# Where table building and the scan's low-rank products stand in an encoder trunk's order of work

## Chip, cores and metric

One core of one Trainium2 chip. The metric is the device time of one execution in microseconds; the median of three runs stands for a kernel.

## What is computed

A trunk of one layer over two independent inputs (batch 0 and batch 1, each 1024 positions of 1024 channels), with the same weights. Each input is normed, projected once, and the columns of the projection go to two mixers: a bidirectional RWKV-7 scan with data-dependent decay, and differential attention. Both are joined by an output projection, a residual and a norm; a gated feed-forward part with a short convolution, a residual and a norm follow. Cut to what matters here:

```python
x = layer_norm(x)
proj = x @ w_in                                  # columns: r, k, v, low-rank rows, gate | q, k, v
pa = pa + mu0 * (shift_prev(pa) - pa) + mu1 * (shift_next(pa) - pa)
w_log = -softplus(-(w0 + tanh(wd) @ decay_up)) - 0.5     # low-rank products, one per direction
a = sigmoid(a0 + ad @ iclr_up)
kk = heads(k * k_k); kk = kk * rsqrt(sum(kk * kk, -1) + 1e-12)      # key norms
y = scan(r, decay, k, v, -kk, kk * a) + the same backwards
lam = exp(sum(lp[0] * lp[1])) - exp(sum(lp[2] * lp[3])) + lam_init
attn = softmax(q0 k0 + bias) - lam * softmax(q1 k1 + bias)          # bias by relative position
x = layer_norm(ALPHA * x + concat(scan part, attention part) @ w_out)
x = layer_norm(ALPHA * x + ffn(x))
```

## The kernel before

All large products are split in two parts of the operands (`hi` rounded, `lo` the rest) and run as three matmuls each: lines 264 to 266 where the weights are the stationary side, lines 288 to 290 where the activations are. The weights of one block of 128 columns come by one load of 512 KB on SP's queue (line 235, through the helper `ld` at line 79, so every DMA of SP shows line 79); ScalarE makes `hi` (line 248) and GpSimd `lo` (line 251).

The program is traced stage by stage, and a scheduler sorts it by priority and by a simulated time into one order per engine, which every engine and every DMA queue then follows strictly. The stages of `run` for batch 0:

- `consts` and `norm_in(0)`: constants, the input norm of batch 0, its transposes into `xT`.
- `columns`: small loads of per-channel parameters, turned by three transposes into `cols`; and behind them, in the same function, tables that only later parts read. These are zeros for the part of the scratch `td` that the inversion does not write (lines 195 to 201, one memset and eight stores; read first by the scan's second pass), lambda as a column (`lamn`, lines 203 to 215, one load, five small operations and a product on TensorE; read by attention), and the bias row by distance (`frow`, lines 217 to 226: one load, 31 copies on GpSimd, two stores; read by attention).
- `project(0)`: fourteen blocks of columns. Block 12 first, the low-rank rows: `shifted` (ScalarE line 396, VectorE lines 397 and 399), a tanh, a split, and four stores into the scratch `stk`. Then block 13 and the gate, and then r, k, v for each of four pairs of heads. From the third pair on, the input norm of batch 1 is woven in.
- `project_qk(0)`, `project_v(0)`: the columns of attention.
- `scan(0)`: `pass1`, `pass2` and `attention`. They have a better priority than the projections, so that the projections fill what the scan leaves.

`pass1` first loads the up-matrices of decay and iclr (line 485, behind the last load of the input of batch 0) and casts them on VectorE (lines 487 to 489). For each half it reads the low-rank rows back from `stk` (line 501, four loads). Then come its local stages, one for each pair and half, eight in a batch. Each (`local`) scales and squares k, sums the squares per head on TensorE (line 539, the key norms) and takes ln and exp on ScalarE (lines 540 and 541); for either direction it forms the decay from a low-rank product (line 549, then tanh at 551, plus one at 552, a scan at 557, two exponentials at 560 and 562) and the learning rate from another (line 554, tanh at 555), builds the operands `AB` (lines 575 to 587), and multiplies them per chunk (line 580). The product of line 599 closes a local stage. `invert` and `merge` follow for each group.

PSUM for these products comes from `spsum`, which gives out two tags in turn, two buffers each: the key norms take one tag, the product of line 549 the other, that of line 554 the first again. Nothing but the operands orders line 549: it needs the rows from `stk` and the up-matrices, not k.

The large tiles of the projections have the tag `t` with seven buffers (shifted outputs, norm rows, and the tables above), and the weights have `w` with four and `whi` with two.

Of the kernel before, what the change touches and what calls it, by code (L numbers as in the profile page):

```python
# [42 lines left out]
class Trunk:  # L43
# [90 lines left out]
    def columns(self):  # L134

        nc, cp, I = self.nc, self.cp, self.I
# [55 lines left out]
        self.cb = cols[:, 300:344]  # L192
        self.rk = cols[:, rows["r_k"] : rows["r_k"] + 4]
        self.WC = self.cs.tile([P, NPAIR, 2, NC2, 2], F32, name="WC")
        self.td = [[self.scr(f"td{g}{h}", [P, 2, 2, NC2, C]) for h in range(2)] for g in range(2)]
        zt = self.dt("t", shape=(32, 4 * NC2, 32))
        nc.vector.memset(zt, 0.0)
# [22 lines left out]
        for b, lo, hi in T5_RANGES:  # L220
            m = 1023 - hi
            nc.gpsimd.tensor_copy(out=fr[m // 1024][:, m % 1024 : m % 1024 + hi - lo + 1],
                                  in_=rb[:, b : b + 1].to_broadcast([4, hi - lo + 1]))
# [5 lines left out]
    def weights(self, w, c0, nk, width=P):  # L229
        nc = self.nc  # L230
        out = []
        for k0 in range(0, nk, 8):
            n = min(8, nk - k0)
            st = self.dt("w", shape=(P, 8, P))
            self.ld(out=st[:, 0:n, 0:width],
                    in_=w[k0 * P : (k0 + n) * P, c0 : c0 + width].rearrange("(k p) c -> p k c", p=P))
            hi, lo = self.dt("whi", F32R, shape=(P, 8, P)), self.dt("w", F32R, shape=(P, 8, P))
            self.split(*(a[:, 0:n, 0:width] for a in (st, hi, lo)))
            out.append((k0, n, hi, lo))
        return out  # L240
# [147 lines left out]
    def project(self, b, between=iter(())):  # L388

        nc, I, S = self.nc, self.I, self.st[b]  # L390

        def shifted(m, width=P):
            pp = self.proj(m * P, width)
            o = self.dt("t")
            w = slice(0, width)
            nc.scalar.activation(out=o[w], in_=pp[w], func=AF.Copy, scale=self.c0[w, m : m + 1])
            nc.vector.scalar_tensor_tensor(out=o[w, 1:T], in0=pp[w, 0 : T - 1], scalar=self.mu[0][w, m : m + 1],
                                           in1=o[w, 1:T], op0=ALU.mult, op1=ALU.add)
            nc.vector.scalar_tensor_tensor(out=o[w, 0 : T - 1], in0=pp[w, 1:T], scalar=self.mu[1][w, m : m + 1],  # L399
                                           in1=o[w, 0 : T - 1], op0=ALU.mult, op1=ALU.add)  # L400
            return o


        o = shifted(12)
        nc.scalar.activation(out=o[0:64], in_=o[0:64], func=AF.Tanh)
        lh, ll = self.dt("t", F32R), self.dt("t", F32R)
        self.hilo(o, lh, ll)
        S["stk"] = self.scr(f"stk{b}", [4, 4, 32, T])
        for g in range(4):
            self.ld(out=S["stk"][:, g], in_=(lh, ll)[g % 2])  # L410
        gd = shifted(13, 96)
        nc.scalar.activation(out=gd[0:96], in_=gd[0:96], func=AF.Tanh, scale=0.5)
        nc.vector.tensor_scalar(out=gd[0:96], in0=gd[0:96], scalar1=0.5, scalar2=0.5, op0=ALU.mult, op1=ALU.add)
        gup = self.dt("t", shape=(96, 512))
        self.ld(out=gup, in_=I["g_up"][0])
        for key in "rk":
            S[key] = [self.scr(f"{key}{b}_{p}", [P, T]) for p in range(NPAIR)]
        S["va"] = self.scr(f"va{b}", [NPAIR, P, T])
        S["g"] = [self.scr(f"g{b}_{p}", [P, T]) for p in range(NPAIR)]

        def gate():
            for p in range(NPAIR):
                pp = self.dpsum()
                for j in range(2):
                    sl = slice(512 * j, 512 * j + 512)
                    nc.tensor.matmul(pp[:, sl], gup[:, p * P : (p + 1) * P], gd[0:96, sl], start=True, stop=True)
                o = self.dt("t")
                nc.scalar.copy(out=o, in_=pp)
                self.ld(out=S["g"][p], in_=o)

        S["v"] = [S["va"][p] for p in range(NPAIR)]
        for p in range(NPAIR):
            for key, m0 in (("r", 0), ("k", 4), ("v", 8)):
                o = shifted(m0 + p)
                self.ld(out=S[key][p], in_=o)
                if p >= 2:
                    with self.ahead():
                        next(between, None)
            if p == 0:
                gate()  # L440
# [31 lines left out]
    def pass1(self, b):  # L472
        nc, I, S = self.nc, self.I, self.st[b]
        S["ab"] = [[self.scr(f"ab{b}_{g}_{h}", [NC2, 2, P, 4, P]) for h in range(2)] for g in range(2)]
        S["p2"] = [[self.scr(f"p2{b}_{p}_{hn}", [P, 512]) for hn in range(2)] for p in range(NPAIR)]
        with self.tc.tile_pool(name=f"p1{b}", bufs=1) as pool:
            def tl(tag, bufs=1, dt=F32, shape=(P, 512)):
                return pool.tile(list(shape), dt, name=self.nm(tag), tag=tag, bufs=bufs)

            ups = []  # L480
            for j, (name, d) in enumerate((("decay_up", 0), ("decay_up", 1), ("iclr_up", 0), ("iclr_up", 1))):
                raw, tmp = tl("kk", 2), tl("sg", 2, F32R)
                src = I[name][0, d]
                with self.tc.issue_after(self.first_loads.ins) if b == 0 else nullcontext():
                    self.ld(out=raw, in_=bass.AP(tensor=src.tensor, offset=src.offset, ap=[[0, 4]] + [list(a) for a in src.ap]))
                up = tl(f"up{j}", dt=F32R)
                nc.vector.tensor_copy(out=up[0:64], in_=raw[0:64])
                nc.vector.tensor_copy(out=tmp[64:128], in_=raw[64:128])
                nc.vector.tensor_tensor(out=up[64:128], in0=raw[64:128], in1=tmp[64:128].bitcast(F32), op=ALU.subtract)
                ups.append(up)  # L490
            smask = tl("smask")
            nc.vector.memset(smask, 1.0)
            nc.vector.memset(smask.rearrange("p (c t) -> p c t", t=C)[:, :, 0:1], 0.0)
            merges, ins, stk = [], [], []

            def load(n):
                if n % 2 == 0 and n < 4:
                    stk.clear()
                    for j in range(4):
                        st = tl(f"stk{j}", dt=F32R)  # L500
                        self.ld(out=st, in_=S["stk"][j, :, :, 256 * n : 256 * n + 512].rearrange("g r t -> (g r) t"))
                        stk.append(st)
                if n < 4:
                    ts = slice(512 * (n // 2), 512 * (n // 2) + 512)
                    for i in range(2):
                        x = {}
                        for key in "krvg":
                            x[key] = tl(key, 3 if key in "kr" else 1)
                            self.ld(out=x[key], in_=S[key][2 * (n % 2) + i][:, ts])
                        ins.append(x)  # L510

            def gap():
                if len(merges) > 1:
                    next(merges[0], None)

            load(0)
            for n in range(4):
                hn, pp = n // 2, n % 2
                abd = [self.scr(f"abd{n % 3}{i}", [C, 2, 2, NC2, C]) for i in range(2)]
                for i in range(2):  # L520
                    self.local(b, 2 * pp + i, hn, tl, ups, stk, smask, abd[i], ins.pop(0), gap)
                if n > 1:
                    merges.pop(0)
                if n == 3:
                    list(merges.pop(0))
                load(n + 1)
                merges.append(self.merge(tl, pp, hn, abd, self.invert(pp, hn, tl, abd, n % 3)))
            list(merges[0])

    def local(self, b, p, hn, tl, ups, stk, smask, abd, x, gap):  # L530
        nc, S = self.nc, self.st[b]
        pc = slice(p * P, (p + 1) * P)
        k, r, v, g = (x[key] for key in "krvg")

        kk, sq = tl("kk", 2), tl("L")
        nc.vector.tensor_scalar(out=kk, in0=k, scalar1=self.kkc[:, p : p + 1], scalar2=0.0, op0=ALU.mult, op1=ALU.add)
        nc.scalar.activation(out=sq, in_=kk, func=AF.Square)
        pn = self.spsum()
        nc.tensor.matmul(pn, self.bones, sq, start=True, stop=True)
        nc.scalar.activation(out=sq, in_=pn, func=AF.Ln, bias=self.bcol[:, 0:1])  # L540
        nc.scalar.activation(out=sq, in_=sq, func=AF.Exp, scale=-0.5, bias=self.bcol[:, 1:2])
        nc.vector.tensor_tensor(out=kk, in0=kk, in1=sq, op=ALU.mult)
# [2 lines left out]
        for d in range(2):  # L545
            h = hn if d == 0 else 1 - hn
            rv = (lambda a: a) if d == 0 else (lambda a: a[:, ::-1])
            pz = self.spsum()
            nc.tensor.matmul(pz, ups[d][:, pc], stk[d], start=True, stop=True)
            sg, ta = tl("sg", 2), tl("ta", 2)  # L550
            nc.scalar.activation(out=sg, in_=pz, func=AF.Tanh, scale=0.5, bias=self.w0h[:, 4 * d + p : 4 * d + p + 1])
            nc.vector.tensor_scalar(out=sg, in0=sg, scalar1=1.0, scalar2=0.0, op0=ALU.add, op1=ALU.add)
# [592 lines left out]
    def run(self, x0, x1, y0, y1):  # L1145
        self.st = {}
        with self.tc.tile_pool(name="cs", bufs=1) as self.cs:
# [8 lines left out]
            self.tc.cur_priority += 100000  # L1156
            between = self.norm_in(1, x1)
            self.project(0, between)
            self.project_qk(0, between)
            for g in range(2):  # L1160
                turn = self.turn_in(1, g)
# [45 lines left out]
```

## Time and profile before

| | us |
|---|---|
| median of 3 runs | 3681.4 (3679.78 to 3683.65) |
| the profiled execution | 3670.72 |
| its span, first to last instruction | 3668.6 |
| TensorE busy | 3351.0 |
| VectorE busy | 1989.5 |
| ScalarE busy | 1421.3 |
| GpSimd busy | 1307.4 |

The profile is that of one execution. The page gives the busy time of each engine (PE TensorE, PEld its weight loads, DVE VectorE, ACT ScalarE, POOL GpSimd, SP the queue that issues most DMAs). A table of stretches cuts the span into pieces. A list of waits says which instruction an engine stood still for and what released it. A timeline lists instructions in order of time.

### The profile page before, as it was taken

How to read it: one execution, taken by the hardware profiler on the slowest of the kernel's cores; microseconds unless marked ns; L12 is line 12 of the kernel's file. 1: busy time of each engine (PE TensorE's matmuls, PEld its weight loads, DVE VectorE, ACT ScalarE, POOL GpSimd, SP SyncE). 2: the span in 40 equal slices, each digit the busy share in tenths (PEclk: the TensorE clock that was granted, in tenths of full speed). 3: DMA queues.
4: the chain of work that ended last, by engine and by line, in shares of the span. 5: the costliest groups of instructions: out<-in, count | busy, mean ns of one | idle time of the engine just before them, and what ended most of it. 6: DMA issues, size and time to landing. Idle time of an engine off the chain costs nothing.

```text
span 3668.6 us, 51545 instructions
## 1 busy us (share of the span) xinstructions
PE 3351.0 (91%) x18981; PEld 2748.6 (75%) x18981; DVE 1989.5 (54%) x3654; ACT 1421.3 (39%) x2477; POOL 1307.4 (36%) x1407
## 2 busy tenths in 40 slices
PE   5788878999999997788999999998998899999997
PEld 4566666788878875566788888876876688888876
DVE  6388762335557865878633345448686633333122
ACT  3234332443335543444334343325454333333222
POOL 5265431000232345544221111345452622222464
PEclk9999879889899998898999999999999999999999
DMA  5568774333364656666643333767654322222642
GB/s 161 167 201 233 210 200 106 119 94 96 108 197 145 210 200 179 165 164 158 141 126 107 95 106 103 239 210 224 189 184 147 115 75 69 75 69 76 223 172 87
DMA packets 605391, 545.31 MB, mean 149 GB/s; under 512 B 207388, under 2 KB 480012, under 8 KB 605140
## 3 DMA queue, kind: packets, MB, share of 16 engines
q1 hardware_dynamic: 538580, 508.45, 45.4%
q10 hardware_dynamic: 66560, 33.56, 3.8%
q8 instruction: 152, 2.49, 0.3%
q14 instruction: 99, 0.81, 0.1%
HBM read 361.49 MB, written 180.39 MB: 148 GB/s over the span
## 4 chain that ended last, share of the span: by engine, by line
PE 66%; DVE 13%; DMA 9%; ACT 3%; issue 3%; POOL 3%; SPq 3%; ACTq 0%; POOLq 0%; DVEq 0%
PE d L264 10%; PE d L266 10%; PE d L265 10%; PE d L288 5%; PE d L289 5%; PE d L290 5%; PE s L745 3%; PE s L813 3%; PE s L795 3%; SPq L79 3%; PE s L805 2%; DVE N L621 1%; PE s L926 1%; DVE Ntmp L619 1%; PE s L927 1%
## 5 line engine op out<-in xcount | busy, mean ns | idle before, releaser
L251 POOL TENSOR_TENSOR w<-w,whi 128x256 fp32r<-128x256 f32 (+1 forms) x800 | 758.2, 974 | 1291.6 <-ACT whi L248 1160.3
L264 PE MATMUL d<-xh,whi 128*128 128x512 f32 (+1 forms) x2112 | 857.4, 406 | 14.8 <-DVE t L399 6.3
L266 PE MATMUL d<-xh,w 128*128 128x512 f32 (+1 forms) x2112 | 851.9, 403 | 2.1 <-POOL w L251 2.1
L265 PE MATMUL d<-xl,whi 128*128 128x512 f32 (+1 forms) x2112 | 849.1, 402 | 0.6 <-DVE xl L308 0.6
L248 ACT ACTIVATE whi<-w 128x512 fp32r<-128x512 f32 (+1 forms) x536 | 308.0, 622 | 752.1 <-PE d L290 232.6
L264 PEld LDWEIGHTS d<-xh,whi 128*128 128x128 f32 (+1 forms) x2112 | 407.2, 193 | 106.0 <-issue 7.5
L266 PEld LDWEIGHTS d<-xh,w 128*128 128x128 f32 (+1 forms) x2112 | 407.0, 193 | 94.2 <-issue 3.5
L265 PEld LDWEIGHTS d<-xl,whi 128*128 128x128 f32 (+1 forms) x2112 | 407.2, 193 | 91.5 <-issue 2.2
L1078 DVE SCALAR_TENSOR_TENSOR t<-d,cols,t 128x1023 f32<-128x1023 f32 x88 | 112.7, 1281 | 405.9 <-ACT t L1077 405.8
L288 PE MATMUL d<-whi,xh 128*128 128x512 f32 x640 | 259.3, 414 | 36.0 <-DVE t L1058 20.7
L289 PE MATMUL d<-w,xh 128*128 128x512 f32 x640 | 261.4, 408 | 2.1 <-POOL w L251 2.1
L290 PE MATMUL d<-whi,xl 128*128 128x512 f32 x608 | 247.0, 406 | 0.0
L1058 DVE SCALAR_TENSOR_TENSOR t<-t,d 128x512 f32<-128x512 f32 x112 | 72.5, 677 | 242.4 <-PE d L290 239.2
L935 ACT ACTIVATE e<-e,ms 128x1024 f32<-128x1024 f32 x128 | 147.0, 1148 | 138.1 <-DVE ms L933 134.4
L288 PEld LDWEIGHTS d<-whi,xh 128*128 128x128 f32 x640 | 124.3, 195 | 71.9 <-issue 12.5
L942 POOL TENSOR_SCALAR e<-e,ms 128x512 f32<-128x512 f32 x128 | 89.0, 708 | 250.0 <-DVE ms L940 108.7
L749 DVE TENSOR_TENSOR G<-s,ms 64x256 f32<-64x256 f32 x128 | 53.7, 420 | 190.8 <-PE s L745 190.1
L289 PEld LDWEIGHTS d<-w,xh 128*128 128x128 f32 x640 | 124.3, 194 | 32.4 <-POOL w L251 5.4
L813 PEld LDWEIGHTS s<-X,Q 128*128 128x128 f32 x1024 | 134.0, 199 | 10.0 <-DVE X L808 1.8
L290 PEld LDWEIGHTS d<-whi,xl 128*128 128x128 f32 x608 | 118.0, 194 | 28.1 <-issue 1.0
L745 PE MATMUL s<-G,BK 64*128 64x128 f32 x1024 | 138.2, 298 | 0.5 <-ACT Q L759 0.3
L813 PE MATMUL s<-X,Q 128*128 128x64 f32 x1024 | 137.1, 280 | 0.3 <-DVE X L808 0.3
(230 smaller groups left out, 6181.6 us busy)
## 6 DMA issues: line engine op xcount, KB each, us to landing
w<-in_ffn_up SPq DMA_DIRECT2D x88, 512.0 KB
w<-in_ffn_down SPq DMA_DIRECT2D x88, 512.0 KB
h<-t SPq DMA_DIRECT2D x66, 512.0 KB
ab<-AB ACTq DMA_DIRECT2D x64, 512.0 KB
w<-in_w_in SPq DMA_DIRECT2D x58, 512.0 KB
G<-ab SPq DMA_DIRECT2D x128, 128.0 KB
BK<-ab SPq DMA_DIRECT2D x64, 256.0 KB
w<-in_w_out SPq DMA_DIRECT2D x32, 512.0 KB
```

What stands on the lines that cost most here:

```text
L248: nc.scalar.activation(out=hi[:, s], in_=w[:, s], func=AF.Copy)
L251: nc.gpsimd.tensor_tensor(out=lo[:, s], in0=w[:, s], in1=hi[:, s].bitcast(F32), op=ALU.subtract)
L264: nc.tensor.matmul(o, wh, rh, start=first, stop=False)
L265: nc.tensor.matmul(o, wh, rl, start=False, stop=False)
L266: nc.tensor.matmul(o, wl, rh, start=False, stop=last)
L288: nc.tensor.matmul(out[i], lh, wh, start=k == ks[0], stop=False)
L289: nc.tensor.matmul(out[i], lh, wl, start=False, stop=False)
L290: nc.tensor.matmul(out[i], ll, wh, start=False, stop=k == ks[-1])
L745: nc.tensor.matmul(pp[i][:, u * P : (u + 1) * P], BK[st, u], G[i][st, u], start=True, stop=True)
L813: last = nc.tensor.matmul(pv[g][:, i, u], ops[g][3][i][:, u], x[:, s, 1, u], start=False, stop=True, skip_group_check=True)
L935: nc.scalar.activation(out=e_, in_=e_, func=AF.Exp, bias=ms[:, 2 + c : 3 + c], accum_out=ms[:, 4 + c : 5 + c])
L1078: nc.vector.scalar_tensor_tensor(out=o[:, 1:T], in0=pp[:, 0 : T - 1], scalar=self.cw[0][:, m : m + 1], in1=o[:, 1:T], op0=ALU.mult, op1=AL ...
```

## The change

Three edits. The tables behind `columns` become a function of their own, `tables`, which `run` calls behind `project(0)`, with the priority of the projections. In `project`, the last load of weights for the first pair's blocks (that of its v block) is kept as `S["ahead"]`, and the loads of the low-rank rows in `pass1` are queued behind it on SP. In `local`, the product of line 549 is queued on TensorE behind the key norms of its stage. `issue_after(ins)` orders what its block traces on the engine of `ins` behind `ins` in the queue of that engine; it adds no wait. No instruction is added or taken away.

```diff
@@ columns
         self.WC = self.cs.tile([P, NPAIR, 2, NC2, 2], F32, name="WC")
+
+    def tables(self):
+
+        nc, cp, I = self.nc, self.cp, self.I
         self.td = [[self.scr(f"td{g}{h}", [P, 2, 2, NC2, C]) for h in range(2)] for g in range(2)]
@@ weights
-            self.ld(out=st[:, 0:n, 0:width],
+            self.loaded = self.ld(out=st[:, 0:n, 0:width],
                     in_=w[k0 * P : (k0 + n) * P, c0 : c0 + width].rearrange("(k p) c -> p k c", p=P))
@@ project
                 o = shifted(m0 + p)
+                if p == 0:
+                    S["ahead"] = self.loaded.ins
                 self.ld(out=S[key][p], in_=o)
@@ pass1, load
-                        self.ld(out=st, in_=S["stk"][j, :, :, 256 * n : 256 * n + 512].rearrange("g r t -> (g r) t"))
+                        with self.tc.issue_after(S["ahead"]):
+                            self.ld(out=st, in_=S["stk"][j, :, :, 256 * n : 256 * n + 512].rearrange("g r t -> (g r) t"))
@@ local
-        nc.tensor.matmul(pn, self.bones, sq, start=True, stop=True)
+        norms = nc.tensor.matmul(pn, self.bones, sq, start=True, stop=True)
@@ local
-            nc.tensor.matmul(pz, ups[d][:, pc], stk[d], start=True, stop=True)
+            with self.tc.issue_after(norms.ins):
+                nc.tensor.matmul(pz, ups[d][:, pc], stk[d], start=True, stop=True)
@@ run
             self.project(0, between)
+            self.tables()
             self.project_qk(0, between)
```

## Rows read from the trace of the kernel before

**Rows 1.** The page's busy line of TensorE: busy us, share, instructions; then the others.

```profile
PE 3351.0 (91%) x18981; PEld 2748.6 (75%) x18981; DVE 1989.5 (54%) x3654; ACT 1421.3 (39%) x2477; POOL 1307.4 (36%) x1407
```

**Rows 2.** Stretches: from:to, us, busy us of each engine, clock, DMA share, GB/s.

```profile
52.00:64.00 12.00, 12.00 (x61) 9.29 (x60) 4.79 (x15) 2.26 (x5) 0.14 (x1) 1.00 0.72 138
64.00:75.00 11.00, 4.11 (x19) 2.68 (x17) 5.46 (x10) 2.35 (x4) 4.12 (x18) 0.91 0.14 45
75.00:90.00 15.00, 12.93 (x42) 9.64 (x42) 6.02 (x5) 5.32 (x6) 9.09 (x23) 0.72 0.33 97
90.00:107.00 17.00, 0.00 (x0) 0.00 (x0) 0.00 (x0) 0.00 (x0) 0.00 (x0) 0.60 0.43 150
...
95.00:103.00 8.00, 0.00 (x0) 0.00 (x0) 0.00 (x0) 0.00 (x0) 0.00 (x0) 0.50 0.25 100
...
107.00:133.00 26.00, 25.85 (x105) 20.98 (x106) 6.05 (x6) 5.79 (x9) 5.67 (x8) 0.93 0.36 118
...
250.00:300.00 50.00, 42.62 (x216) 33.69 (x215) 49.51 (x74) 18.67 (x26) 28.89 (x28) 0.86 0.74 215
300.00:350.00 50.00, 36.73 (x220) 28.28 (x219) 34.83 (x54) 18.60 (x26) 28.04 (x28) 0.89 0.84 235
```

**Rows 3.** Waits of TensorE, 60 to 115 us: us in total, times, longest.

```profile
PE s L549 <- DMA stk<-stk: 17.2, 1, 17.2
PE d L264 <- DVE t L399: 6.3, 1, 6.3
PE d L266 <- POOL w L251: 1.7, 1, 1.7
```

**Rows 4.** Timeline of SP's queue: start, us of issuing, what is moved, how many.

```profile
53.25 7.95 SPq L79 DMA_DIRECT2D td<-t  x8
...
61.79 1.19 SPq L79 DMA_DIRECT2D kk<-in_iclr_up  x2
...
74.91 0.25 SPq L79 DMA_DIRECT2D frow<-t  x1
75.25 0.41 SPq L79 DMA_DIRECT2D w<-in_w_in  x1
77.45 7.28 SPq L79 DMA_DIRECT2D stk<-t  x4
...
91.16 0.42 SPq L79 DMA_DIRECT2D w<-in_w_in  x1
103.74 1.77 SPq L79 DMA_DIRECT2D stk<-stk  x4
```

**Rows 5.** Timelines of ScalarE, VectorE and GpSimd, 64 to 80 us.

```profile
65.88 1.09 ACT L396 ACTIVATE t<-d,c 128x1024 f32<-128x1024 f32 x1
...
71.27 1.29 DVE L489 TENSOR_TENSOR up<-kk,sg 64x512 fp32r<-64x512 f32 x2
72.59 1.28 DVE L397 SCALAR_TENSOR_TENSOR t<-d,cols,t 128x1023 f32<-128x1023 f32 x1
...
70.88 6.65 POOL L222 COPY t<-t 4x1 f32<-4x1 f32 x31 [18.74 <-DMA t<-in_rel_bias]
```

**Rows 6.** The longest wait of ScalarE, 80 to 115 us.

```profile
ACT sg L551 <- PE s L549: 22.8, 1, 22.8
```

**Rows 7.** Timeline of the first two local stages: decay, next early product, next norms.

```profile
141.18 0.70 ACT L551 ACTIVATE sg<-s,halfc 128x512 f32<-128x512 f32 x1
...
143.90 0.41 DVE L552 TENSOR_SCALAR sg<-sg 128x512 f32<-128x512 f32 x1
...
159.62 0.79 PE L549 MATMUL s<-stk,up 128*128 128x512 f32 x1
...
187.87 1.02 PE L539 MATMUL s<-L,bones 128*128 128x512 f32 x2
188.33 0.80 PE L554 MATMUL s<-stk,up 128*128 128x512 f32 x1
```

**Rows 8.** A wait of TensorE from 1380 to 1860 us, first pass of batch 1.

```profile
PE s L549 <- ACT L L540: 5.9, 1, 5.9
```

## The prediction

> **What bounds the kernel now.** I read the page's busy line first: TensorE is busy for 91% of the span [rows 1], and the work that it does hardly changes here, so the question is where it stands idle. A table of stretches then shows that the first 107 us are the worst part: from 64 to 75 us TensorE works 4.11 of 11 us, from 75 to 90 it works at a mean clock of 0.72, and from 90 to 107 no engine does anything at all [rows 2]. A stretch in which all five engines are empty is time that can be taken out whole, since nothing else fills it. The list of waits says for what TensorE stood still there: 17.2 us before the first low-rank product of the scan (line 549), for the load of its operand; 6.3 us before the third projection, for VectorE's shift (line 399); 1.7 us for GpSimd's split of the weights [rows 3]. The order on SP's queue explains the operand: the low-rank rows are stored from 77.45 us, and the load that reads them back leaves at 103.74, when the store has landed [rows 4]. Line 549 stood ahead of the k projection in TensorE's order, so that a projection whose weights had been fetched from 75.25 us on waited for a product that nobody needed yet. ScalarE, whose queue is in order too, stood 22.8 us behind that product with the split of the next weights behind it [rows 6].
>
> **Part 1: the tables leave the head.** Eight stores of zeros (7.95 us of SP), the load and arithmetic of lambda, the load of the bias table, 31 small GpSimd copies (6.65 us) and two stores of the bias row go from before the first projection to behind its last column block. What goes with them:
> - The two iclr_up loads issue at 61.79 us, right behind the eight stores that begin at 53.25 [rows 4]. VectorE's casts of them end with line 489 at 71.27 + 1.29 us, and only then comes the shift of the first projection, line 397 at 72.59, whose input ScalarE had finished at 65.88 + 1.09 = 66.97 [rows 5]. With the loads some 8 us earlier the casts are done by about 65 and the shift begins at 66.97: 72.59 - 66.97 = 5.6 us, inside the 6.3 us for which TensorE waited. I take **5.6**. Of that wait 0.7 us stays: the shift is then itself what comes last.
> - GpSimd is at the 31 copies from 70.88 to 77.5 us [rows 5] while the split that the third projection needs stands behind them: **1.7 us** [rows 3].
>
> **Part 2: the first low-rank product goes behind the key norms.** Line 549 is now queued behind line 539, which needs k from the projection that it used to hold up. So it can't stand ahead of that projection any more, and its operand is there before it is asked for: **17.2 us** [rows 3]. The whole of it counts, since no engine worked meanwhile [rows 2].
>
> **The clock.** Behind both idle stretches TensorE ran below full speed: 15 us at 0.72 and 26 us at 0.93, after 0.60 in the empty stretch [rows 2]; 0.72 lies between its two levels, 1.2 and 2.4 GHz. If all of that were won back it would be 15 x 0.28 + 26 x 0.07 = 6 us; if a new gap of 2 us keeps the lower level for a time, nothing. I take **3**, the middle.
>
> Sum of the gains: 5.6 + 1.7 + 17.2 + 3 = **27.5 us**.
>
> **What it costs.**
> - **The tables at their new place.** I take it that tiles of one tag are handed out in the order of the program, and so expect them behind the outputs of the last v block, at about 290 us in the old times. The stretch is full: VectorE 49.51 of 50 us before 300, the DMA engines 0.84 from 300 to 350, and TensorE idle 13.3 us of those 50 already [rows 2]. All twelve DMAs stand in SP's queue between weight loads, the stores of the bias row wait for GpSimd's copies, and what is queued behind them on SP waits along: weights, and so TensorE. The lower bound is 0, as the scan does not need the tables before its second pass and a gain is excluded (the stretch loses no work); the upper is both rows one after the other, 7.95 + 6.65 = 14.6 us [rows 4, 5]. I take **5**, nearer to the lower, as TensorE can run one projection ahead there and much of what it waits for is VectorE.
> - **The products behind the norms.** There are 16 local stages (two batches, four steps, two pairs). Until now line 549 ran ahead: at 159.62 us, with its norms at 187.87 [rows 7], so its decay (lines 551 and 552) was done long before it was wanted. Now the product (0.79), ScalarE's line 551 (0.70) and VectorE's line 552 (0.41) lie behind the norms [rows 7], beside the two activations of the norms. Upper bound: 16 x 1.90 = 30 us. Lower bound: -5.9 us, since the early products also made TensorE wait, 5.9 us in the second batch [rows 8]. I take **2**: the decay has until the key is normed, and dense products fill TensorE meanwhile.
> - **Loads behind the weights of the v block.** These stood in that order anyway: the load of v's weights at 91.16, that of the low-rank rows at 103.74 [rows 4]. So the new order on SP only keeps what is there. But the store takes 103.74 - 77.45 = 26.3 us, and with the shift it starts at about 71.8 and lands at 98. By then r is done (69.7 + 12) and k too, at about 93. If v's weights are issued behind the store and wait for it, TensorE stands up to 5 us; if ahead, nothing. I take **2.5**, the middle.
>
> One rule on that store: by the Trainium skill, DMA: Bandwidth & Descriptors, section "Why a DMA increments its semaphore by 16 and not by 1", a copy runs on the largest number of engines up to 16 that divides the slowest dimension of both sides, which is 4 for this store. The row from 95 to 103 us, with nothing else in flight, agrees: a share of 0.25 and 100 GB/s [rows 2]. By the rule the landing stays at 98 and so does the 2.5; were it free to spread, 2 MB at the 235 GB/s of rows 2 would land near 81, and the sum would be 2.5 better.
>
> A rule that speaks against the change: the same page, section "Specifications", asks for at least 512 bytes in a piece, and the zeros are stored in pieces of 128. The rows agree so far: a share of 0.72 for 138 GB/s while they run, 0.84 for 235 later [rows 2]. By it the stores take 0.72 x 12 = 8.6 us of all engines wherever they stand, and the 16% that are free from 300 to 350 are 8 us: estimated so, the price of the new place would be 8.6 and not 5.
>
> **The sum.** 27.5 - 5 - 2 - 2.5 = **18 us**. The profiled execution took 3670.7 us (its span 3668.6 and 2.1 around it), so 3652.7; the median of the runs is 10.7 above that execution, and the same 18 us from 3681.4 give **3663.4**. What the measurement can tell from no change is about 0.2%, 7.4 us.
>
> **The rivals.**
> - **The tables stall the later stretch as they did the head.** For: it is fuller than the head was, and a store that waits for GpSimd holds SP again. Against: the weights are fetched ahead. At 14.6 us and with the clock term gone: 27.5 - 3 - 14.6 - 4.5 = 5.4, **3676**, within 0.2%.
> - **The scan becomes the bound: slower.** Each local stage is a chain over TensorE, ScalarE and VectorE, and VectorE is full from 250 to 300 us [rows 2]. If the 1.90 us of line 549 and its decay come on top of each chain and TensorE waits for it, 30 us go: 27.5 - 5 - 30 - 2.5 = -10, **3691**. It decides from 20 / 16 = 1.25 us per stage on. Against it: TensorE has other work in most of these stages.
> - **It doesn't do what it says.** Only line 549 is tied to the norms; line 554 reads the same kind of operand and isn't. If it is put ahead of the k projection instead, the 17.2 us and 2 of the clock stay: **3682**. Against it: in the trace it runs right behind the norms, at 188.33 after 187.87 [rows 7], and it shares their PSUM tag.
> - **All costs at their lower ends:** 27.5 + 5.9 = 33, **3648**.
>
> **How the numbers follow.** The forecast (3663; its own range 3652 to 3673, the middles of clock, tables, products and loads off by up to 3, 5, 5 and 2.5 us but not all one way) has 0.50, the lower ends 0.10, the later stall 0.17, the scan as bound 0.13, no effect on the wait 0.10. From 3644 to 3688 lie all but the slower case and a few per cent below. Faster: 0.50 + 0.10 + a quarter of the stall = 0.64. Same: the rest of the stall and most of the fourth, 0.21. Slower: 0.15.
>
> **What would show it.** The wait of line 549 for its load gone, and no stretch up to 110 us with all engines empty; the shift of line 397 at about 67 us; the first norms (134 us before) at 105 to 110. Wrong would be: another product waiting for the same load, a gap of over 10 us behind the stores of zeros near 270 us, or TensorE idle longer in either first pass of the scan.

## The result and the profile after

The forecast was 3663.0 us, range 3644 to 3688. The change is slower, and outside that range:

| | before | after |
|---|---|---|
| median, us | 3681.25 (3679.78 to 3683.65, 4 runs) | 3730.99 (3727.94 to 3733.29, 4 runs) |
| ratio | 1 | 1.0134 (95%: 1.0116 to 1.0152) |
| profiled execution: span, mean granted clock | 3668.6, 0.943 | 3726.2, 0.931 |

Lines of after are 4 higher than those of before from about line 195 on, and 7 or 8 higher in and behind `local`: L546 are the key norms (before: 539), L557 the low-rank product that the change ties to them (549), L562 the other one (554), L588 the chunk products (580), L655 the inversion's (647), L217 lambda's product (213), L268 to L270 the dense products of the projections (264 to 266). Each run below has line numbers of its own again.

TensorE's stretches after, to be read against [rows 2]; columns are from:to, us, busy us (instructions), granted clock, DMA share, GB/s:

```profile
52.00:64.00 12.00, 5.28 (x22) 0.86 0.27 93
64.00:75.00 11.00, 11.00 (x42) 0.84 0.05 13
75.00:90.00 15.00, 12.77 (x50) 0.89 0.36 102
90.00:107.00 17.00, 17.00 (x76) 1.00 0.24 99
107.00:133.00 26.00, 14.26 (x34) 0.66 0.56 182
133.00:250.00 117.00, 117.00 (x498) 0.99 0.56 173
250.00:300.00 50.00, 42.67 (x228) 0.93 0.73 219
600.00:700.00 100.00, 55.29 (x632) 0.53 0.46 96
```

and two stretches of before that are not among its rows above:

```profile
133.00:250.00 117.00, 104.38 (x531) 0.99 0.67 203
600.00:700.00 100.00, 87.72 (x541) 0.80 0.42 123
```

The empty stretch from 90 to 107 us is gone, as forecast. Instead TensorE waits before 64 us and from 107 to 133; it is busy without a break from 133 to 250, where before it had gaps; and from 600 to 700 it stands idle for 44.7 us, where before it was 12.3, with the clock near the lower of its two levels (1.2 of 2.4 GHz).

What it did in the full stretch says where the loss begins. TensorE's timeline after, from the first key norms on (start, us, instruction, count, idle time before it and what ended it; `issue` where the profile names no releaser):

```profile
120.79 3.75 PE L430 MATMUL d<-t,t 96*128 96x512 f32 x4 [8.31 <-issue]
127.54 2.08 PE L546 MATMUL s<-L,bones 128*128 128x512 f32 x2 [3.00 <-ACT L L544]
128.63 1.42 PE L562 MATMUL s<-stk,up 128*128 128x512 f32 x1
130.48 3.78 PE L430 MATMUL d<-t,t 96*128 96x512 f32 x4 [0.44 <-ACT t L432]
133.28 1.42 PE L557 MATMUL s<-stk,up 128*128 128x512 f32 x1
...
249.25 0.38 PE L217 MATMUL s<-t,bcol 1*128 1x1 f32 x2
249.55 0.50 PE L557 MATMUL s<-stk,up 128*128 128x512 f32 x1
...
259.84 1.15 PE L588 MATMUL s<-AB 64*64 64x64 f32 x32
```

The first norms run at 127.54, 6.6 us ahead of before (134.1), and line 557 follows for one direction at 133.28. For the other direction the same product runs only at **249.55**, right behind lambda's product at 249.25. The first chunk products come at 259.84, where before they came at 147.72: the scan starts 112 us late. From 138.2 us to lambda's product TensorE does only projections. In SP's queue the load of lambda's parameters stands at 238.50 us, behind the input of batch 1: its tile has the tag `t`, and the program asks for it behind those of the projection.

The waits of TensorE from 0 to 700 us (us in total, times, longest), first the largest of after, then its like in before:

```profile
PE s L655 <- DMA M<-t1d: 45.7, 5, 12.9
```

```profile
PE s L647 <- DMA M<-t1d: 14.1, 2, 12.1
```

At the end of the first pass TensorE waits 45.7 us for the inversion's data, with nothing else to do: the projections that fill those gaps in before have already run, and the next ones aren't let go yet. A helper, `paced`, orders the projections of batch 1 behind marks in the scan of batch 0, so that they run at most a set amount of work ahead of it (50 us). From 133 us to the first norms of batch 1 (1421.5 us before, 1456.7 after) TensorE is idle for 125.1 us before and 159.5 after, which is where most of the loss lies:

```profile
133.00:1421.50 1288.50, 1163.45 (x7207) 0.91 0.57 166
```

```profile
133.00:1456.70 1323.70, 1164.25 (x7185) 0.89 0.56 161
```

### The profile page after: what moved, and what is told of

It reads as the page before. It is cut to its first block, busy times and chain, and to the rows that moved or that the text cites. A ratio compares the mean times of both kernels' runs of the same rounds, so it can differ in the third digit from the quotient of the medians.

```text
span 3726.2 us, 51564 instructions
## 1 busy us (share of the span) xinstructions
PE 3368.0 (90%) x18981; PEld 2767.3 (74%) x18981; DVE 1988.6 (53%) x3654; ACT 1419.2 (38%) x2475; POOL 1308.6 (35%) x1407
## 5 line engine op out<-in xcount | busy, mean ns | idle before, releaser
L268 PE MATMUL d<-xh,whi 128*128 128x512 f32 (+1 forms) x2112 | 856.1, 406 | 9.8 <-ACT whi L252 5.0
L270 PE MATMUL d<-xh,w 128*128 128x512 f32 (+1 forms) x2112 | 842.5, 399 | 0.4 <-POOL w L255 0.4
L268 PEld LDWEIGHTS d<-xh,whi 128*128 128x128 f32 (+1 forms) x2112 | 404.4, 192 | 102.2 <-ACT whi L252 7.9
L270 PEld LDWEIGHTS d<-xh,w 128*128 128x128 f32 (+1 forms) x2112 | 403.6, 191 | 93.4 <-issue 2.4
L943 ACT ACTIVATE e<-e,ms 128x1024 f32<-128x1024 f32 x128 | 147.0, 1149 | 138.4 <-DVE ms L941 119.4
L950 POOL TENSOR_SCALAR e<-e,ms 128x512 f32<-128x512 f32 x128 | 89.3, 711 | 219.2 <-DVE ms L948 124.6
L753 PE MATMUL s<-G,BK 64*128 64x128 f32 x1024 | 146.0, 305 | 10.9 <-DMA v<-va 10.7
L293 PEld LDWEIGHTS d<-w,xh 128*128 128x128 f32 x640 | 124.6, 195 | 31.6 <-POOL w L255 4.0
L753 PEld LDWEIGHTS s<-G,BK 64*128 64x128 f32 x1024 | 121.3, 204 | 31.5 <-issue 22.3
```

The source lines that it names most:

```text
L268: nc.tensor.matmul(o, wh, rh, start=first, stop=False)
L270: nc.tensor.matmul(o, wl, rh, start=False, stop=last)
L293: nc.tensor.matmul(out[i], lh, wl, start=False, stop=False)
L753: nc.tensor.matmul(pp[i][:, u * P : (u + 1) * P], BK[st, u], G[i][st, u], start=True, stop=True)
L943: nc.scalar.activation(out=e_, in_=e_, func=AF.Exp, bias=ms[:, 2 + c : 3 + c], accum_out=ms[:, 4 + c : 5 + c])
```

## Experiments

Each ratio is to before's runs on the same chip, with its 95% interval. "Products behind the norms" is the third edit of the change (lines 549 and 539), "loads behind weights" the second.

**1. Lambda alone moved.** The kernel before with only lambda's lines (203 to 215) traced behind `project(0)`; zeros and bias row stay at the head, and no ordering is added.

> The kernel before, with nothing changed but the place of lambda: its load, its arithmetic and its product go behind the first projection; the zeros, the bias row and both orderings stay as before. Theory A (the product's PSUM tile stands ahead of the scan's tiles of the same tag, so the low-rank product of the first local stage waits for lambda, whose tiles come behind the projection's): the product of lambda and behind it the first low-rank product of direction 0 run at about 250 us, the first chunk products at about 260 instead of 148, and the time is 3725 to 3740, all of the loss of the change. Theory B (the zeros and the bias row stall the stretch where they land, or the orderings lengthen the local stages): 3675 to 3685, as before.

3722.0 us, ratio 1.0102 (1.0077 to 1.0126). Just under the 3725 to 3740 expected. Its TensorE timeline shows the same pair, lambda's product (L227) and the scan's low-rank product (L552):

```profile
247.43 0.38 PE L227 MATMUL s<-t,bcol 1*128 1x1 f32 x2
247.73 0.50 PE L552 MATMUL s<-stk,up 128*128 128x512 f32 x1
```

Moving a load, five small operations and one product (0.38 us, two instructions) is enough for about 39 of the 50 us.

**2. Everything but lambda.** The changed kernel with lambda's lines left in `columns`.

> The changed kernel with lambda left where it was, ahead of the first projection: zeros and bias row move, both orderings stay. Theory A: the loss goes away and what was forecast for the head comes: first norms at 105 to 115 us, no wait for the low-rank rows, 3650 to 3675. Theory B: the loss stays, 3715 to 3735, as zeros, bias row and orderings are all still there.

3687.0 us, 1.0012 (0.9992 to 1.0033): the loss is gone, but what was forecast for the head does not come, so the 3650 to 3675 expected are missed.

**3. Lambda moved, its product in another PSUM tag.** The changed kernel with

```diff
-        pl = self.spsum()
+        self.side = not self.side
+        pl = self.dpsum()
```

so that only the tile's tag differs: `d`, that of the projections. The first of the two lines keeps the turn of the scan's two tags as it was.

> The changed kernel with one thing other: lambda's product writes a PSUM tile of the projections' tag instead of one of the scan's; all tables stay moved. Theory A: the same as with lambda left at its place, 3650 to 3675, since the tag alone was the matter. If it is not the tag but the late arithmetic of lambda: 3725 to 3740.

3680.8 us, 0.9989 (0.9970 to 1.0008): the same miss of 3650 to 3675, and the loss gone again. Lambda's product now runs at 307.9 us, later than ever, and the scan doesn't care (L547 norms, L558 the tied product, now for both directions at once):

```profile
126.19 2.07 PE L547 MATMUL s<-L,bones 128*128 128x512 f32 x2 [2.82 <-ACT L L545]
127.27 1.42 PE L558 MATMUL s<-stk,up 128*128 128x512 f32 x1
128.49 0.63 PE L563 MATMUL s<-stk,up 128*128 128x512 f32 x1
129.13 3.78 PE L431 MATMUL d<-t,t 96*128 96x512 f32 x4
131.92 1.42 PE L558 MATMUL s<-stk,up 128*128 128x512 f32 x1
```

Runs 1 to 3 settle the loss. Tiles of a PSUM tag are handed out in the order in which the program asks for them. Lambda's product asks before the scan, so the scan's first product of that tag can't have a tile until lambda's has had one. The tag has two buffers, one for each of the two products, and line 557 ran right behind lambda's product without waiting for its result to be read: it was held by the order of handing out, not by a lack of room. That the product of the other direction, of the other tag, ran at 133.28 fits.

**4. The tables moved, no ordering.** The changed kernel without its second and third edit.

> The tables moved as in the change, without its two orderings: the low-rank loads aren't held behind weight loads and the products aren't held behind the norms. Theory (lambda's product takes a PSUM tile of the scan's two tags and holds the scan's first direction-0 product behind it): the loss stays whole, 3720 to 3740 us, that product at about 249 us instead of 147.7, and 600 to 700 us as empty for TensorE as in the changed kernel (about 45 us idle). Rival (the loss needs an ordering too, since a product held behind the norms can't run early): 3680 to 3695.

3707.9 us, 1.0082 (1.0054 to 1.0109): about half of the loss stays (26 of 50 us), below the 3720 to 3740 expected, with TensorE busy 56.75 us of the 100 from 600 to 700. The loss does not need the orderings, but they make it some 24 us larger here.

**5. The changed kernel with projections further ahead.**

```diff
-FREE = (50.0, 1e9)
+FREE = (110.0, 1e9)
```

> The changed kernel with the second batch's projections allowed to run 110 us of work ahead of the first batch's scan instead of 50, lambda's product where the change puts it. Theory (the late scan costs what TensorE then lacks in work: the projections are tied to the scan's progress and are not let go while it catches up): TensorE idle from 600 to 700 us about 20 to 35 us instead of 45, and 3700 to 3720. Rival (the loss is the scan's own length from its first product to its end, whatever runs beside it): 3725 to 3740 with the stretch as empty as before.

3701.4 us, 1.0054 (1.0028 to 1.0081). The stretch that was empty is full again:

```profile
600.00:700.00 100.00, 94.47 (x802) 0.91 0.54 131
```

From 133 us to batch 1's first norms TensorE is idle for 135.0 us, against 159.5 in the changed kernel:

```profile
133.00:1428.40 1295.40, 1160.36 (x7171) 0.91 0.56 163
```

So 112 us of late start cost 50 us at the end largely because TensorE ran short of other work while the scan caught up; about 30 of them come back with more work let go. The kernel before was not run with the same 110 us, so how much of the 30 it would win there too is not shown.

**6. Only the two orderings.** The kernel before with the second and third edit.

> The kernel before with the two orderings alone; all tables stay at the head. By the terms of the prediction: the 17.2 us wait goes and about 2 us of the clock come back, less 2 for the later decay and 2.5 for the loads, 3660 to 3672. By theory B (the orderings lengthen each of 16 local stages by up to 1.9 us): 3685 to 3712.

3683.7 us, 1.0001 (0.9984 to 1.0018). Neither range expected (3660 to 3672, 3685 to 3712) has it. The wait of 17.2 us is gone and the first norms come at 125.7 instead of 134.1, with nothing of it at the end. Runs 2, 3 and 6 have this in common, and it opened the second question: where does the gain of the head go?

**7 and 8. The product behind the norms in the first local stage alone**, in the kernels of runs 6 and 2:

```diff
-            with self.tc.issue_after(norms.ins):
+            with self.tc.issue_after(norms.ins) if b == 0 and p == 0 and hn == 0 else nullcontext():
```

> The kernel before with the two orderings, that of the product behind the norms for the first local stage alone (batch 0, first pair, first step); the tables at the head as before. In the run with the ordering in every stage the first norms came 8 us earlier and the second batch's norms 15 us earlier, and the end was not earlier. Theory (the ordering in the later stages gives the head's gain back, in the second batch's first pass and at its attention): 3664 to 3674, with attention of the second batch starting 10 us or more ahead of before. Rival (the gain is lost around the start of the second batch's attention however the stages are ordered): 3680 to 3686.

> The changed kernel with lambda left where it was and the ordering of the products behind the norms for the first local stage alone. Theory (later stages' ordering gives the gain back): the first norms at 120 us as with all stages ordered, second batch's norms some 20 us ahead of before, and 3656 to 3670. Rival (gain lost at the second batch's attention anyway): 3680 to 3688.

3673.9 us, 0.9984 (0.9966 to 1.0001), and 3671.7 us, 0.9977 (0.9958 to 0.9996). Both move the expected way; the first lies at the upper end of its range, the second just above, and only the second interval excludes 1. Batch 1's attention does not start 10 us earlier in run 7, as expected, but at 2480.7 us (before: 2477.4). TensorE's idle time tells how large the head's gain is: up to 133 us it is 54.9 us in before, 47.0 in run 7, 48.8 in run 6 and 46.8 in run 2. That is 6 to 8 us, beside a clock of 0.92 instead of 0.90. In run 7 the medians differ by 8 us too.

**9 and 10. Weights, then k too, ahead of the low-rank loads.** Run 8 with those loads also behind the weights of the next pair's r; then also behind the store of k.

> The one before, with the low-rank loads held behind the weight load of the next pair's r too, so that those weights are not queued behind them on SP. If the 9 us that TensorE waited from 104 to 114 us come from weights queued behind low-rank loads that wait for their store: the first norms at 110 to 114 us and 5 to 9 us less than the run before at all later marks, 3648 to 3664. If they come from ScalarE's and VectorE's order (a split ahead of k's shift): norms at 118 to 121 and the same time as the run before within 3 us.

> As the run before it (lambda where it was, products behind the norms in the first local stage alone, low-rank loads behind the next pair's weights) and the low-rank loads also behind the store of k, so that k too is not queued behind loads that wait for the long store. Theory (whatever stands behind the four low-rank loads on SP waits until the store lands at about 99 us; it was the weights, then the key): the first norms at 109 to 113 us instead of 118 to 120, the first product some 2 us behind, and the end 3655 to 3668. Rival (the key's way to the norms is set by ScalarE's and VectorE's order): norms at 116 to 120 and no less time than 3664 to 3672.

3666.9 us, 0.9973 (0.9955 to 0.9991), and 3668.9 us, 0.9971 (0.9950 to 0.9992): the same as run 8 within the intervals, and run 9 above the 3648 to 3664 expected. The traces show a wait that moves along a queue. SP's queue in run 2, where the low-rank loads come first (start, us of issuing):

```profile
73.23 7.55 SPq L79 DMA_DIRECT2D stk<-t  x4
...
99.31 1.77 SPq L79 DMA_DIRECT2D stk<-stk  x4
101.13 0.43 SPq L79 DMA_DIRECT2D w<-in_w_in  x1
```

and what waited there, on ScalarE:

```profile
ACT whi L252 <- DMA w<-in_w_in: 25.6, 2, 24.3
```

The weights for the next block sit behind loads that wait for the long store, ScalarE's split of them sits ahead of k's shift, and TensorE idles 9.25 us before 113.57. In run 9 the weights go first and TensorE idles 2.1 us there, but 8.5 us before the norms (2.9 in run 2), since VectorE now waits for k, whose load is the one behind:

```profile
DVE kk L543 <- DMA k<-k: 10.4, 1, 10.4
```

In run 10 k is ahead as well; its wait is still 8.1 us, and the norms come at 116.0 (run 8: 120.0, run 9: 118.0). The expectations of 110 to 114 (run 9) and 109 to 113 (run 10) were not met. What won 18 us against before at the first norms is worth 5.8 at the first product of the second pass's chain (line 795 in before; 636.2 against 642.0). TensorE's longest waits from 250 to 600 us (the chunk products, for their operands `AB`), before and run 10, show where the rest went:

```profile
PE s L580 <- DVE AB L576: 26.6, 8, 6.1
```

```profile
PE s L590 <- DVE AB L586: 44.3, 9, 7.6
```

TensorE arrives earlier and waits 17.7 us longer for VectorE's operands; over the whole stretch it is busy for 11.2 us less (277.82 against 289.01).

**11 and 12. The orderings in one batch only**: run 6 with the products behind the norms for batch 0 alone (`if b == 0`; the loads stay behind the weights in both batches), and with both orderings for batch 1 alone.

> The kernel before with the two orderings, the products behind the norms in the first batch only. Theory (the cost of the ordering falls in the second batch's first pass, where TensorE waits for VectorE's decay): from the first batch's attention to the second's 1425 to 1436 us as before, and 3664 to 3676 in all. Rival (the cost is in both batches): 3676 to 3684.

> The kernel before with both orderings in the second batch only, so the head is that of before. Theory: from the first batch's attention to the second's 1440 to 1450 us instead of 1427.6, TensorE idle some 15 us longer between 1390 and 1700, and 3690 to 3700 in all. Rival (the ordering costs nothing there, the head's gain is lost by other means): 3679 to 3686.

3653.9 us, **0.9919** (0.9902 to 0.9937), and 3692.8 us, 1.0025 (1.0009 to 1.0041). The ordering costs in batch 1, 8 to 9 us in run 12, as the theory had it. But batch 0 alone gains 31 us, far more than the 6 to 18 expected. TensorE's order in run 11 is that of run 6, instruction by instruction, up to the first local stage of batch 1: the ordering in batch 1 is all that was taken away, and the two medians differ by 30 us (the two profiled executions by 18). TensorE from 1400 to 1700 us, in before, run 6 and run 11:

```profile
1400.00:1700.00 300.00, 237.71 (x1495) 0.85 0.63 165
1400.00:1700.00 300.00, 223.85 (x1450) 0.84 0.60 156
1400.00:1700.00 300.00, 228.02 (x1433) 0.82 0.63 162
```

and its longest wait there, that of the chunk products for their operands `AB`, in run 6 and in run 11:

```profile
PE s L584 <- DVE AB L580: 45.7, 10, 13.3
```

```profile
PE s L584 <- DVE AB L580: 25.3, 8, 5.9
```

With the ordering, TensorE waits 20 us longer for the operands that come out of the decay: the low-rank product that used to run ahead of the norms now lies behind them, and the decay with it. But other waits make up for most of that, as TensorE is busy for only 4.2 us more in run 11. Stretches cut at the same products, and not at the same times, show where the two part. First batch 1's first pass (first norms to the first product of the second pass), then its attention (first to last product of lines 926 and 927 in before), in before, run 6, run 11 and run 12:

```profile
1421.50:1872.10 450.60, 386.49 (x2790) 0.89 0.60 153
1406.20:1862.40 456.20, 381.16 (x2775) 0.88 0.58 149
1416.30:1862.20 445.90, 373.82 (x2710) 0.87 0.60 150
1431.20:1880.00 448.80, 377.24 (x2771) 0.89 0.61 151
```

```profile
2477.40:2812.00 334.60, 313.74 (x1555) 0.97 0.60 193
2475.50:2816.40 340.90, 319.34 (x1592) 0.97 0.61 192
2450.50:2802.20 351.70, 342.53 (x1725) 0.98 0.64 202
2496.70:2835.40 338.70, 319.57 (x1592) 0.96 0.62 193
```

In the first pass TensorE is idle for 64.1 us in before, 75.0 in run 6, 72.1 in run 11 and 71.6 in run 12. So the ordering in batch 1 is paid there: 7.5 us more in run 12 than before, about what it measured. That pass also takes back what run 6 had won in the head. Run 11 does not get it back there (72.1). Its gain lies in the attention, 9.2 us idle against 21.6 in run 6 and 20.9 in before: more dense products (lines 288 to 290) were left to fill that stretch, 842 against 744 in run 6 and 696 in before. Why the scheduler leaves more of them there is not shown.

**13 to 15. The change without its fault, batch 0 alone.** Run 2, run 3 and run 10 with the products behind the norms in batch 0 only.

> The changed kernel with lambda left where it was and the ordering behind the norms in the first batch alone. With that ordering in both batches it measured 1.0012 of before. Theory (the ordering in the second batch gives the gain back, 9 to 31 us): 3650 to 3668. Rival (the ordering in the second batch matters only with the tables at the head, by the order that the planner then finds): 3676 to 3690, as with both batches.

> The changed kernel with lambda's product in the projections' PSUM tiles and the ordering behind the norms in the first batch alone. With both batches it measured 0.9989 of before. Theory: 3650 to 3668. Rival: 3674 to 3686, as with both batches.

> As the first of these, with the low-rank loads behind the next weights and k's store, which made the first norms come at 116.0 us instead of 120.0. If time won in the first stage reaches the end: 2 to 4 us less than the first of these. If the scan's later stages are held by other work and TensorE just waits for VectorE there (44.3 us instead of 26.6 between 250 and 600 in the run with the first stage alone ordered): the same within 4 us.

3672.2 us, 0.9997 (0.9977 to 1.0017); 3652.5 us, **0.9943** (0.9920 to 0.9965); 3678.0 us, 1.0002 (0.9986 to 1.0018). Run 14 met its expectation, 13 and 15 did not. Leaving the ordering out of batch 1 moved all three pairs the same way (runs 6 to 11: 1.0001 to 0.9919; 3 to 14: 0.9989 to 0.9943; 2 to 13: 1.0012 to 0.9997, which the intervals don't separate), but by 5 to 30 us. Run 15, whose first norms are the earliest of all (115.2), is no faster than run 13 (119.4) and clearly slower than run 11 (126.3). All four kernels with the products ordered in every stage of batch 0 alone (runs 11, 13, 14, 15) have the full attention of run 11: 8 to 10 us idle, against 19 to 24 in the others apart from run 5 (15.5). Run 15 loses it again before: from 133 us to batch 1's first norms TensorE is idle for 139.7 us, against 124.6 in run 11. So a few us won in the first stage are easily outweighed by how the scheduler sorts the later stages. Between runs 11 and 13 the traces show only 3 us of idle time up to the end of that attention, while the medians differ by 18 us: this stays open. Runs 11 and 14 beat both kernels.

## Why the prediction was wrong

**The step that failed** is the cost of the tables at their new place (5 us, bounds 0 and 14.6). It named the rule that did the damage, tiles of one tag are handed out in the order of the program, and applied it to the tag `t` alone. The moved function also asks for a PSUM tile, of the tags that the scan's products use; both lines are in the kernel (212 and 548). Following "the scan does not need the tables before its second pass" was right for the data and wrong for the buffer. By the same, what is said ahead of the prediction, that nothing but its operands orders line 549, does not hold: its PSUM tile orders it too. None of the rivals had it: the bound of 14.6 for this step stands against 45 to 53 us measured (1.0134 against 1.0012 and 0.9989 in runs 2 and 3). Without this fault the forecast would have missed too: those two runs are no faster than before, so the 18 us did not come.

**The head's gains** were 27.5 us in the sum; TensorE's idle time up to 133 us fell from 54.9 to 49.6. By term:
- *The shift, 5.6 us.* The shift was to begin at 66.97 us and begins at 74.95. The iclr loads were indeed earlier (54.71 us), but VectorE's casts moved with them, and two of them, waiting for their load, now stand ahead of the split of batch 0's input that TensorE's first projection needs. VectorE after, and TensorE behind it:

```profile
60.41 0.42 DVE L493 CAST up<-kk 64x512 fp32r<-64x512 f32 x1 [5.87 <-DMA kk<-in_iclr_up]
60.84 0.42 DVE L494 CAST sg<-kk 64x512 fp32r<-64x512 f32 x1
61.30 0.69 DVE L312 TENSOR_TENSOR xl<-s,xh 128x512 fp32r<-128x512 f32 x1
```

```profile
62.05 0.80 PE L269 MATMUL d<-xl,whi 128*128 128x512 f32 x1 [5.00 <-DVE xl L312]
```

  The forecast asked when the casts would be done, not what is queued behind them while they wait. In run 2 short operations of lambda sit there instead, the split runs at 56.93 and the shift begins at 68.35.
- *The copies, 1.7 us.* Right: no wait for GpSimd's split is left there.
- *The wait of line 549, 17.2 us.* It is gone, as are the 22.8 us of ScalarE behind it [rows 6]; instead ScalarE stands 23.4 us for weights. About half of it came back as the gap before the gate's products (8.31 us after, 9.25 in run 2). This is the term "loads behind the weights of the v block", 2.5 us: it looked at v's weights, and the ones that waited were those behind the low-rank loads on SP. The long store itself was as forecast, 26.1 us from issue to the loads behind it (80.18 to 106.25 after, 73.23 to 99.31 in run 2) against 26.3 before [rows 4]. By the Trainium skill, DMA: Bandwidth & Descriptors, section "Why a DMA increments its semaphore by 16 and not by 1", a copy runs on the largest number of engines up to 16 that divides the slowest dimension of both sides, 4 for this store; the unchanged time agrees.
- *The clock, 3 us.* It did not come: 0.66 from 107 to 133 us, where before it was 0.93 [rows 2], since the idle time moved there, and 0.90 over the first 133 us in both.
- *The zeros.* The Trainium skill, DMA: Bandwidth & Descriptors, section "Specifications", asks for pieces of at least 512 bytes, by which the stores would have cost 8.6 us, an estimate of the forecast. No run shows that price, but the ratios alone can't exclude it: with the tables moved but lambda mended, 1.0012 and 0.9989 stand beside 1.0001 without the move, each to about 0.2%. From 133 us to batch 1's first norms TensorE is idle for 124.1 us with the zeros moved (run 2) and 122.8 without (run 6).

So the norms came at 127.5, and not at 105 to 110.

**The products behind the norms**, 2 us with bounds -5.9 and 30. The rival that made this the bound had the right mechanism in the second batch: run 12 measured 8 to 9 us for it (with the loads' ordering there), and its trace has 7.5 us more idle time in that pass, against the 2 us forecast. Run 11 against run 6 measured 30 us, but most of that lies in the attention, which no term of the forecast covers. The bound of 30 itself counted 16 products; line 549 runs for two directions, 32 times. The reason given, that dense products fill TensorE meanwhile, doesn't hold from 1400 on, where TensorE was busy for only 237.7 of 300 us already in before.

**What was right:** the wait of line 549 and the empty stretch are gone, and line 554 did not take its place: the rival "it doesn't do what it says" fell. So did the stall behind the stores of zeros: in the changed kernel they leave from 239.11 us on, in the stretch without a gap. And "TensorE idle longer in the first pass", named as a sign of being wrong, is what the profile shows.

## What to carry to other kernels

A step that is moved takes its place in every queue that it uses, and a buffer tag is such a queue: list the tiles that the moved lines ask for, by tag, PSUM included, and ask who asks next. When an early wait is taken away, look one place further down the same queue before counting the gain, and ask whether the later work is held by something else. Compare stretches between the same instructions, by the idle time in them, and not between the same times. Where a scheduler sorts anew after every edit, judge a gain of 10 us in one place from several kernels that share it, not from one.

## What the runs showed of the hardware

One and the same kernel, that of before, took between 3662.2 and 3698.6 us over 26 runs on one chip, with a mean granted clock of 0.947 in the fastest and 0.935 in the slowest. In the trace of before, steps of the clock are to be seen in the second pass:

```profile
700.00:720.00 20.00, 20.00 (x162) 1.00 0.26 71
720.00:740.00 20.00, 17.35 (x113) 0.88 0.43 118
740.00:760.00 20.00, 20.00 (x89) 0.50 0.14 48
```

TensorE idled 2.65 us, then ran at the lower level for 20 us while busy throughout, which is some 10 us of work lost. That the short wait set this off is not shown; it came just before. Executions drift apart without any difference in their order: runs 6 and 11 have the same order on every compute engine up to the first local stage of batch 1, and TensorE reaches the place where its orders part at 1386.8 us in one and at 1397.1 in the other. So times in late places are compared here by the idle time of a stretch, or where several kernels agree.
